# Attention and mixer's output: product A12 B21 first, block sums spread over the products, two-tensor operations on VectorE

## The chip, the cores and the metric

The kernel runs on one core of one Trainium2 chip. The metric is the time of one execution in microseconds, as the device measures it. The profile is of one execution; its engines are TensorE (PE, its weight loads PEld), VectorE (DVE), ScalarE (ACT), GpSimd (POOL) and SyncE (SP, which only issues transfers here).

## What is computed

A decoder trunk of two layers over 1024 positions of width 1024, all in float32. Each layer is a mixer, a cross-attention to 256 memory tokens and a SwiGLU FFN, and after each of the three stands a layer norm of the residual sum:

```python
def memory_cross_attention(x, mem_n, w_q, w_k, w_v, w_o):
    ...
    s = jnp.einsum('bshd,bmhd->bhsm', q, k).astype(jnp.float32) * (XA_DH ** -0.5)
    p = jax.nn.softmax(s, axis=-1).astype(x.dtype)
    o = jnp.einsum('bhsm,bmhd->bshd', p, v).reshape(B, S, D_MODEL)
    return o @ w_o

def swiglu_ffn(x, w_gate, w_up, w_down):
    return (jax.nn.silu(x @ w_gate) * (x @ w_up)) @ w_down

def reference(...):
    ...
    for l in range(DEPTH):
        if l % 2 == 0:
            ...
            y = hybrid_ab_mixer(x, ...)          # ends with y @ w_out
        else:
            ...
            y = multiscale_pool_mixer(x, ...)
        x = layer_norm(ALPHA * x + y, ln_mix_g[l], ln_mix_b[l])
        y = memory_cross_attention(x, mem_n, xa_wq[l], xa_wk[l], xa_wv[l], xa_wo[l])
        x = layer_norm(ALPHA * x + y, ln_xa_g[l], ln_xa_b[l])
        y = swiglu_ffn(x, ffn_wg[l], ffn_wu[l], ffn_wd[l])
        x = layer_norm(ALPHA * x + y, ln_ffn_g[l], ln_ffn_b[l])
    return x
```

## The kernel before, in words

**Precision.** Every operand of a product is split in two: a hi part, which ScalarE casts (L215, weights L123), and a lo part, the operand minus its hi part, a two-tensor subtraction on VectorE or GpSimd (L216, weights L125; `w.lo_engine` says which engine takes the weights' lo parts). One product is then three matmuls into the same bank (`mm3`, L210 to L212).

**Attention.** The kernel doesn't form q, k, v and o one by one. `build_A` multiplies the query weight with the memory's keys into a matrix A of 1024 x 1024, `attn_scores` multiplies x with it, a softmax follows, `build_VWo` multiplies the memory's values with the output weight, and `attn_out` multiplies the probabilities with that. So the scores, the attention's output and the mixer's output of the first layer are each a product of 1024 x 1024 by 1024 x 1024.

**Seven products.** Such a product is done in 2 x 2 blocks of 512 with seven block products in place of eight (`seven`, L807). With A blocks A11, A12, A21, A22 and B blocks in the same manner, product 1 is A11 B11, product 2 is A12 B21, and products 3 to 7 have block sums as operands (S1 to S4 of the A blocks, T1 to T4 of the B blocks). `ORDER_A` gives their order. A block is two pages of 128 x 1024, and a product has two halves g of one page of each side; a half product has 24 matmuls, 4 row tiles p of 6. `operands7` makes the hi and lo parts of each half product in that order, some three or four halves ahead, and `hook(j, g)`, called ahead of each half, issues the block sums (`combos_A`, `combos_B`), loads of x and layer-norm pieces.

**Banks.** The products accumulate in PSUM, in sets of four banks. Products 1, 6, 7 and 4 go on in one set (each adds to what stands there), 5 and 3 in another, and 2 in a set of its own. There are eight banks. So a new set needs banks of a finished one, and after each product the four results are added to the residual tiles x (L247 on VectorE; in the scores a VectorE addition or a ScalarE copy). Product 4 accumulates in the bank that product 7's addition has read, so it waits for that addition.

**Order.** Nothing is scheduled by a planner: the instructions stand on each engine's queue as the program emits them, and each engine does them in turn. `add` follows a product, `hook` precedes a half, and the operands' parts come between. The page pool has 44 pages; a page is taken again when its last reader is done.

**On which engine.** GpSimd takes the lo parts of A, many block sums (L732, L737, L741, L745, L757, L761), the weights' lo parts in the mixer's output, the attention's output and FFN-down, the softmax scaling of tiles 1 to 7 (L939; tile 0 has four VectorE operations, L942), and in FFN-down the affine step of tiles 4 to 6 (L1371, L1372). VectorE takes the lo parts of B, the other sums, the additions, and two operations for each tile of a layer norm (`ln_b`, L262 and L263). FFN-down has seven products too, in another order (`ORDER_D`) and with a different source for its operands; the first layer's weight transfers for it are issued by SyncE behind the stores of ScalarE that it waits for.

Of the kernel before, what the change touches and what calls it, by code (L numbers as in the profile page):

```python
# [15 lines left out]
P = 128  # L16
# [20 lines left out]
ORDER_A = (1, 2, 5, 6, 3, 7, 4)  # L37
ORDER_D = (1, 5, 6, 3, 7, 4, 2)

# [12 lines left out]
AFFINE = {(1, 2): ((0, "vector"), (4, "gpsimd")), (1, 3): ((1, "vector"),), (1, 4): ((2, "vector"), (5, "gpsimd")),  # L52
          (1, 5): ((3, "vector"),), (5, 1): ((6, "gpsimd"),), (5, 3): ((7, "vector"),)}
# [91 lines left out]
class Kern:  # L145
# [430 lines left out]
    def out_operands(self):  # L576

        A, B = {}, {}
        for k in (1, 2):
# [3 lines left out]
        A[1] = [self.Y[0, 0, g] for g in range(2)]  # L583
# [4 lines left out]
    def mixer0_out(self):  # L588
# [22 lines left out]
        def hook(j, g):  # L611
            if j == 1:
                if g == 0:
                    while self.y_ready[2] < 4:
                        self.pump()
                    A[2] = Y(0, 1)
# [25 lines left out]
        self.w.lo_engine = ("gpsimd",)  # L642
# [82 lines left out]
    def combos_A(self, A, step, eng):  # L725

        tt = eng.tensor_tensor
        if step == 0:
            (A11, A12), (A21, A22) = A["blocks"]
            S1 = [self.page("S1", [2, 512]) for _ in range(2)]  # L730
            for g in range(2):
                tt(S1[g], A21[g], A22[g], op=ALU.add)  # L732
            A.update({1: A11, 2: A12, 4: A22, 5: S1})
        elif step == 1:
            A11, S3 = A[1], A.pop("blocks")[1][0]
            for g in range(2):
                tt(S3[g], A11[g], S3[g], op=ALU.subtract)  # L737
            A[7] = S3
        elif step == 2:
            for g in range(2):  # L740
# [883 lines left out]
```

## Time and profile before

| | before |
|---|---|
| median of the runs | 2451.51 us (3 runs, 2450.9 to 2452.84) |
| profiled execution | 2451.65 us, its span 2449.9 us |
| mean granted clock of TensorE | 0.976 |
| busy: TensorE | 2312.4 us, 94% of the span |
| busy: VectorE, ScalarE, GpSimd | 1778.0, 1044.2 and 665.9 us |

How to read what follows: a time line gives the start of an instruction, its duration and, in brackets, how long its engine had stood idle before it and who ended that. A wait line gives the waiting engine's tile and line, the releaser, the us in total, the number of times and the longest. A window line gives the stretch, its us, the busy time (and instructions) of PE, PEld, DVE, ACT and POOL, the granted clock (1.00 is full), the DMA share and GB/s. A group of instructions has its busy time, the mean ns of one and the idle time before them. Short names: D is the set of banks of the seven products, dh and dl the hi and lo parts of their operands, S and T block sums, B a block of the right side, y and wp the mixer's left and right side, xf a block of x transposed, x a residual tile, wh and wl a weight's parts, pa and pk banks of `build_A` and the second mixer, xt a bank for transposes, s and hf sums of FFN-down's left side, p softmax tiles.

### The profile page before, as it was taken

How to read it: one execution, taken by the hardware profiler on the slowest of the kernel's cores; microseconds unless marked ns; L12 is line 12 of the kernel's file. 1: busy time of each engine (PE TensorE's matmuls, PEld its weight loads, DVE VectorE, ACT ScalarE, POOL GpSimd, SP SyncE). 2: the span in 40 equal slices, each digit the busy share in tenths (PEclk: the TensorE clock that was granted, in tenths of full speed). 3: DMA queues.
4: the chain of work that ended last, by engine and by line, in shares of the span. 5: the costliest groups of instructions: out<-in, count | busy, mean ns of one | idle time of the engine just before them, and what ended most of it. 6: DMA issues, size and time to landing. Idle time of an engine off the chain costs nothing. (4 is left out here: it accounts for less than half of the span.)

```text
span 2449.9 us, 29443 instructions
## 1 busy us (share of the span) xinstructions
PE 2312.4 (94%) x11208; PEld 1916.5 (78%) x11208; DVE 1778.0 (73%) x2126; ACT 1044.2 (43%) x1727; POOL 665.9 (27%) x401
## 2 busy tenths in 40 slices
PE   8999997797979999999999989798999999999998
PEld 7777776696868888888878789786788888887886
DVE  6986788868795876766774566978767667676555
ACT  3245555344736544444412234546364444342212
POOL 1332346757483000000110073755610000002001
PEclk9999999899989999999999999999999999999999
DMA  5111124050122234435796642302024353449783
GB/s 185 69 35 35 35 90 160 26 187 28 53 77 87 95 130 163 159 125 184 280 356 230 247 142 102 118 1 103 36 85 158 126 182 130 161 176 392 261 291 117
DMA packets 117341, 344.02 MB, mean 140 GB/s; under 512 B 10832, under 2 KB 11344, under 8 KB 117200
## 3 DMA queue, kind: packets, MB, share of 16 engines
q1 hardware_dynamic: 70560, 244.35, 27.7%
q10 hardware_dynamic: 46640, 97.79, 11.1%
q8 instruction: 89, 1.46, 0.2%
q14 instruction: 52, 0.43, 0.1%
HBM read 239.34 MB, written 102.76 MB: 140 GB/s over the span
## 5 line engine op out<-in xcount | busy, mean ns | idle before, releaser
L210 PE MATMUL P<-xh,op 128*128 128x512 f32 x1120 | 436.2, 389 | 2.1 <-ACT u L1301 2.1
L212 PE MATMUL P<-xh,op 128*128 128x512 f32 x1120 | 435.7, 389 | 0.0
L211 PE MATMUL P<-xl,op 128*128 128x512 f32 x1120 | 435.7, 389 | 0.0
L210 PE MATMUL D<-dh,dl 128*128 128x512 f32 x560 | 226.2, 404 | 58.4 <-DVE x L247 35.4
L1371 POOL TENSOR_TENSOR x<-x,lng 128x1024 f32<-128x1024 f32 x6 | 17.9, 2980 | 867.8 <-DVE s L1179 421.4
L210 PE MATMUL D<-dh,wp 128*128 128x512 f32 x616 | 242.4, 394 | 9.5 <-ACT dh L215 8.3
L210 PEld LDWEIGHTS P<-xh,op 128*128 128x128 f32 x1120 | 210.2, 188 | 47.3 <-ACT u L1301 3.8
L211 PE MATMUL D<-dl,wp 128*128 128x512 f32 x616 | 243.0, 395 | 3.3 <-DVE dl L216 3.3
L1113 DVE TENSOR_TENSOR op<-raw,op 128x512 fp32r<-128x512 f32 x200 | 137.9, 689 | 147.5 <-ACT op L1112 147.5
L212 PEld LDWEIGHTS P<-xh,op 128*128 128x128 f32 x1120 | 210.2, 188 | 44.0
L211 PE MATMUL D<-dl,dh 128*128 128x512 f32 x560 | 224.6, 401 | 21.1 <-DVE dl L216 21.1
L211 PEld LDWEIGHTS P<-xl,op 128*128 128x128 f32 x1120 | 210.2, 188 | 43.3
L212 PE MATMUL D<-dh,wp 128*128 128x512 f32 x616 | 241.8, 393 | 0.0
L212 PE MATMUL D<-dh,dh 128*128 128x512 f32 x560 | 223.4, 399 | 0.0
L125 POOL TENSOR_TENSOR wl<-raw,wh 128x1024 fp32r<-128x1024 f32 x64 | 173.5, 2723 | 164.3 <-ACT wh L123 159.9
L216 DVE TENSOR_TENSOR dl<-wp,dh 128x1024 fp32r<-128x1024 f32 x96 | 127.6, 1336 | 115.9 <-ACT dh L215 72.8
L215 ACT CAST dh<-wp 128x1024 fp32r<-128x1024 f32 x96 | 93.8, 989 | 265.4 <-DVE wp L777 57.3
L365 DVE SCALAR_TENSOR_TENSOR cacc<-sig,par,cacc 128x1023 f32<-128x1023 f32 (+14 forms) x120 | 175.5, 1462 | 2.5
L210 PEld LDWEIGHTS D<-dh,dl 128*128 128x128 f32 x560 | 108.8, 194 | 85.5 <-issue 36.6
L257 POOL TENSOR_SCALAR lst<-lst 128x1 f32<-128x1 f32 x48 | 27.3, 568 | 466.7 <-ACT sq L256 466.3
L216 POOL TENSOR_TENSOR dl<-xf,dh 128x1024 fp32r<-128x1024 f32 x48 | 141.5, 2965 | 39.6 <-ACT dh L215 29.2
L216 DVE TENSOR_TENSOR dl<-B,dh 128x1024 fp32r<-128x1024 f32 x48 | 117.9, 2488 | 40.7 <-ACT dh L215 40.7
(272 smaller groups left out, 5236.6 us busy)
## 6 DMA issues: line engine op xcount, KB each, us to landing
wp<-hD SPq DMA_DIRECT2D x140, 512.0 KB, 5.8
hD<-sh ACTq DMA_DIRECT2D x66, 512.0 KB, 3.8
raw<-in_wg SPq DMA_DIRECT2D x44, 512.0 KB, 4.2
raw<-in_wu SPq DMA_DIRECT2D x44, 512.0 KB, 3.3
hD<-hf ACTq DMA_DIRECT2D x44, 512.0 KB, 3.7
hD<-s ACTq DMA_DIRECT2D x44, 512.0 KB, 4.6
wp<-in_wd SPq DMA_DIRECT2D x40, 512.0 KB, 7.8
xD<-x ACTq DMA_DIRECT2D x32, 512.0 KB, 3.8
```

What stands on the lines that cost most here:

```text
L125: eng.tensor_tensor(lo, raw, hi.bitcast(F32), op=ALU.subtract)
L210: mm(out, ll, rh, start=start, stop=False, skip_group_check=more)
L211: mm(out, lh, rl, start=False, stop=False, skip_group_check=more)
L212: mm(out, lh, rh, start=False, stop=stop, skip_group_check=more)
L215: self.nc.scalar.copy(hi, src)
L216: getattr(self.nc, lo_engine).tensor_tensor(lo, src, hi.bitcast(F32), op=ALU.subtract)
L257: nc.gpsimd.tensor_scalar(st[:, 3:4], st[:, 3:4], 1.0 / D, LN_EPS, op0=ALU.mult, op1=ALU.add)
L365: nc.vector.scalar_tensor_tensor(acc[:, s:], u[:, :S - s], w[:, j:j + 1], acc[:, s:], op0=ALU.mult, op1=ALU.add)
L1113: getattr(nc, lo_engine).tensor_tensor(pg[:, 1], src, pg[:, 0].bitcast(F32), op=ALU.subtract)
L1371: eng.tensor_tensor(x[t], x[t], gx[0], op=ALU.mult)
```

## The change

`ORDER_A` begins with product 2 in place of product 1, and the residual's first term goes with it (`add_block` has an argument `early`, which FFN-down sets to 1 as before). The eight block sums have a table `SUMS`, which names the half product ahead of which each is issued: two operations of 128 x 1024 each, all on VectorE. No sum is issued while A or the value-output product is built. There the weight columns come in the order 4 to 7, 0 to 3, so that the blocks of product 2 are made first, and three halves of operands are made ahead. All lo parts of operands, the weights' lo parts in the three stages named, the softmax scaling and the affine step are on VectorE. VectorE's list goes from 2,021 rows to 2,189 and GpSimd's from 406 to 238; GpSimd keeps the weights' lo parts of the first mixer's projections and operations on single columns.

```diff
-ORDER_A = (1, 2, 5, 6, 3, 7, 4)
+ORDER_A = (2, 1, 5, 6, 3, 7, 4)
 ORDER_D = (1, 5, 6, 3, 7, 4, 2)
+
+SUMS = {(2, 1): "S1", (1, 0): "T1", (1, 1): "T2", (5, 0): "S2", (5, 1): "S3", (6, 0): "S4", (6, 1): "T3", (3, 1): "T4"}
...
-AFFINE = {(1, 2): ((0, "vector"), (4, "gpsimd")), (1, 3): ((1, "vector"),), (1, 4): ((2, "vector"), (5, "gpsimd")),
-          (1, 5): ((3, "vector"),), (5, 1): ((6, "gpsimd"),), (5, 3): ((7, "vector"),)}
+AFFINE = {(1, 2): (0, 4), (1, 3): (1,), (1, 4): (2, 5), (1, 5): (3,), (5, 1): (6,), (5, 3): (7,)}
...
         def hook(j, g):
-            if j == 1:
+            if j == 2:
...
-                B[("12", 3)[g]] = take2()
-                if g == 1:
-                    self.combos_B(B, 0, nc.vector)
-                    self.combos_B(B, 1, nc.gpsimd)
-            if j == 2 and g == 0:
+                B[(3, "12")[g]] = take2()
+            if j == 1 and g == 0:
                 while self.bg or self.bg2:
                     self.pump()
-                A["blocks"] = ((A[1], A[2]), (Y(1, 0), Y(1, 1)))
-                for i in range(3):
-                    self.combos_A(A, i, nc.vector)
-                self.combos_B(B, 2, nc.gpsimd)
-            if (j, g) in ((2, 1), (5, 0)):
+                A.update({"21": Y(1, 1), 4: Y(1, 0)})
+                self.block_sum(A, B, "S1")
+            if j != 2 and (j, g) in SUMS:
+                self.block_sum(A, B, SUMS[j, g])
+            if (j, g) in ((1, 1), (5, 0)):
                 load(4 + 2 * (j == 5))
                 load(5 + 2 * (j == 5))
-            if j == 6 and g == 0:
-                self.combos_B(B, 3, nc.vector)
-                self.combos_A(A, 3, nc.gpsimd)
...
-        self.w.lo_engine = ("gpsimd",)
+        self.w.lo_engine = ("vector",)
...
-    def operands7(self, order, fa, fb, ng, fast=()):
+    def operands7(self, order, fa, fb, ng):
         for j in order:
             for g in range(ng):
                 r = []
-                for f, eng in ((fa, "vector" if (j, g) in fast else "gpsimd"), (fb, "vector")):
+                for f in (fa, fb):
                     src = f(j, g)
                     hi, lo = self.page("dh", list(src.shape[1:]), F32R), self.page("dl", list(src.shape[1:]), F32R)
-                    self.split(hi, lo, src, eng)
+                    self.split(hi, lo, src)
...
-    def add_block(self, j, b, x0, x1, s0, s1):
+    def add_block(self, j, b, x0, x1, s0, s1, early=2):
...
-        x, st, eh, first = {1: (x0, None, 0, True), 2: (x0, s0, 0, False), 6: (x0, None, 1, True), 3: (x0, s0, 1, False),
+        x, st, eh, first = {early: (x0, None, 0, True), 3 - early: (x0, s0, 0, False), 6: (x0, None, 1, True), 3: (x0, s0, 1, False),
...
-        if pool:
-            nc.gpsimd.tensor_tensor(p, p, rs.unsqueeze(2).broadcast_to([P, HEADS, MEM]), op=ALU.mult)
-            return
         for h in range(HEADS):
             nc.vector.tensor_scalar(p[:, h, :], p[:, h, :], rs[:, h:h + 1], None, op0=ALU.mult)
...
         def attn(l):
-            for i in range(8):
+            for i in (4, 5, 6, 7, 0, 1, 2, 3):
                 w.add(a["wqT"][l, i], [8, P])
-            for i in range(8):
+            for i in (4, 5, 6, 7, 0, 1, 2, 3):
                 w.add(a["xa_wo"][l, i * P:(i + 1) * P, :], [D])
```

The new function that issues a sum, `block_sum(A, B, name)`, ends with two VectorE operations, one for each page:

```python
        for g in range(2):
            self.nc.vector.tensor_tensor(r[g], a[g], b[g], op=op)
```

In the order lists below, a line number of the changed kernel is one more for the same operation (L247 is L248, L216 is L217, L262 is L263), and L752 is a block sum there.

VectorE's list at the opening of the mixer's output, before: from the last of product 1's additions (x<-x,D) over three sums (two operations each, the second of each left out) and two lo parts to the additions of product 2.

```order
L247 SCALAR_TENSOR_TENSOR x_3513<-x_3513,D_514_3478 128x512
L732 TENSOR_TENSOR S_527_3561<-y_1538,y_3302 128x1024
...
L737 TENSOR_TENSOR y_1538<-y_1400,y_1538 128x1024
...
L741 TENSOR_TENSOR y_1400<-y_3302,y_1538 128x1024
...
L216 TENSOR_TENSOR dl_3580<-wp_435_3116,dh_3579 128x1024
L216 TENSOR_TENSOR dl_3616<-wp_461_3235,dh_3615 128x1024
L247 SCALAR_TENSOR_TENSOR x_3469,lst_3461<-x_3469,D_529_3571 128x512
L247 SCALAR_TENSOR_TENSOR x_3471,lst_3462<-x_3471,D_530_3572 128x512
L247 SCALAR_TENSOR_TENSOR x_3511,lst_3463<-x_3511,D_531_3573 128x512
L247 SCALAR_TENSOR_TENSOR x_3513,lst_3464<-x_3513,D_532_3574 128x512
```

The same place in the changed kernel: the additions are now those of product 2, the first of the stage.

```order
L217 TENSOR_TENSOR dl_3520<-y_3004,dh_3519 128x1024
L217 TENSOR_TENSOR dl_3524<-wp_480_3353,dh_3523 128x1024
L248 SCALAR_TENSOR_TENSOR x_3469<-x_3469,D_511_3475 128x512
L248 SCALAR_TENSOR_TENSOR x_3471<-x_3471,D_512_3476 128x512
L248 SCALAR_TENSOR_TENSOR x_3511<-x_3511,D_513_3477 128x512
L248 SCALAR_TENSOR_TENSOR x_3513<-x_3513,D_514_3478 128x512
L752 TENSOR_TENSOR S_525_3555<-y_3302,y_1538 128x1024
...
L752 TENSOR_TENSOR wp_470_3291<-wp_486_3372,wp_470_3291 128x1024
...
L217 TENSOR_TENSOR dl_3566<-S_525_3555,dh_3565 128x1024
L217 TENSOR_TENSOR dl_3570<-wp_470_3291,dh_3569 128x1024
L752 TENSOR_TENSOR T_535_3597<-wp_482_3364,wp_470_3291 128x1024
```

The six operations of sums that stood between the first and the second product's additions are gone from there; product 2's additions stand behind lo parts alone, and each sum comes between the lo parts of later halves.

VectorE's list at the end of the mixer's output, before: from product 3's last addition over two tiles' layer norm, one lo part, and two more tiles' to the first of product 7's additions (x_3607).

```order
L247 SCALAR_TENSOR_TENSOR x_3513,lst_3464<-x_3513,D_548_3654 128x512
...
L262 SCALAR_TENSOR_TENSOR x_3469<-x_3469,lst_3461,lng_3457 128x1024
L263 SCALAR_TENSOR_TENSOR x_3469<-x_3469,lst_3461,lnb_3458 128x1024
...
L216 TENSOR_TENSOR dl_3906<-wp_480_3353,dh_3905 128x1024
L262 SCALAR_TENSOR_TENSOR x_3511<-x_3511,lst_3463,lng_3457 128x1024
L263 SCALAR_TENSOR_TENSOR x_3511<-x_3511,lst_3463,lnb_3458 128x1024
L262 SCALAR_TENSOR_TENSOR x_3513<-x_3513,lst_3464,lng_3457 128x1024
L263 SCALAR_TENSOR_TENSOR x_3513<-x_3513,lst_3464,lnb_3458 128x1024
L247 SCALAR_TENSOR_TENSOR x_3607,lst_3465<-x_3607,D_511_3475 128x512
```

The same place in the changed kernel.

```order
L256 TENSOR_SCALAR lst_3464<-lst_3464 128x1
L263 SCALAR_TENSOR_TENSOR x_3469<-x_3469,lst_3461,lng_3457 128x1024
L264 SCALAR_TENSOR_TENSOR x_3469<-x_3469,lst_3461,lnb_3458 128x1024
...
L126 TENSOR_TENSOR wl_578_3892<-raw_3473,wh_577_3891 128x1024
L217 TENSOR_TENSOR dl_3902<-y_2644,dh_3901 128x1024
L217 TENSOR_TENSOR dl_3906<-wp_461_3235,dh_3905 128x1024
L263 SCALAR_TENSOR_TENSOR x_3511<-x_3511,lst_3463,lng_3457 128x1024
L264 SCALAR_TENSOR_TENSOR x_3511<-x_3511,lst_3463,lnb_3458 128x1024
L263 SCALAR_TENSOR_TENSOR x_3513<-x_3513,lst_3464,lng_3457 128x1024
L264 SCALAR_TENSOR_TENSOR x_3513<-x_3513,lst_3464,lnb_3458 128x1024
L126 TENSOR_TENSOR wl_584_3938<-raw_3515,wh_583_3937 128x1024
L248 SCALAR_TENSOR_TENSOR x_3601,lst_3465<-x_3601,D_527_3561 128x512
```

Between the additions of product 3 and of product 7 stand three operations more: the A side's lo part (dl<-y) and two weights' lo parts (wl).

VectorE's list at the start of the first score stage, before: sums of the B blocks, then the lo parts of four half products' B side, then the first VectorE additions to the score tiles p.

```order
L752 TENSOR_TENSOR B_4434<-B_4436,B_4434 128x1024
...
L757 TENSOR_TENSOR T_691_4742<-B_4582,B_4434 128x1024
...
L761 TENSOR_TENSOR B_4436<-B_4582,B_4436 128x1024
...
L216 TENSOR_TENSOR dl_4757<-B_4580,dh_4756 128x1024
L216 TENSOR_TENSOR dl_4789<-B_4581,dh_4788 128x1024
L216 TENSOR_TENSOR dl_4833<-B_4434,dh_4832 128x1024
L216 TENSOR_TENSOR dl_4865<-B_4435,dh_4864 128x1024
L971 TENSOR_TENSOR p_4816<-D_709_4824,p_4816 128x512
```

The same place in the changed kernel, from the first sum of the stage on.

```order
L752 TENSOR_TENSOR S_697_4768<-xf_4293,xf_4295 128x1024
...
L217 TENSOR_TENSOR dl_4773<-xf_4153,dh_4772 128x1024
L217 TENSOR_TENSOR dl_4777<-B_4577,dh_4776 128x1024
L752 TENSOR_TENSOR B_4576<-B_4578,B_4576 128x1024
...
L217 TENSOR_TENSOR dl_4819<-S_697_4768,dh_4818 128x1024
L217 TENSOR_TENSOR dl_4823<-B_4576,dh_4822 128x1024
L752 TENSOR_TENSOR T_715_4850<-B_4436,B_4576 128x1024
...
L217 TENSOR_TENSOR dl_4855<-S_698_4769,dh_4854 128x1024
L217 TENSOR_TENSOR dl_4859<-B_4577,dh_4858 128x1024
L947 TENSOR_TENSOR p_4804<-D_707_4814,p_4804 128x512
```

The sums stood together, ahead of the lo parts; now each pair of sums is followed by the two lo parts (A's and B's) of one half product or of two.

## Rows read from the trace of the kernel before

**Rows 1.** The page's engines: busy us (share of the span) x instructions

```profile
PE 2312.4 (94%) x11208; PEld 1916.5 (78%) x11208; DVE 1778.0 (73%) x2126; ACT 1044.2 (43%) x1727; POOL 665.9 (27%) x401
```

**Rows 2.** TensorE's waits: line, releaser, us in total, times, longest

```profile
PE D L210 <- DVE x L247: 35.4, 6, 14.8
PE D L211 <- DVE dl L216: 24.4, 7, 10.6
PE D L210 <- POOL dl L216: 23.0, 5, 9.6
PE D L210 <- ACT dh L215: 8.3, 2, 4.1
PE pk L210 <- POOL wl L125: 6.1, 3, 5.7
PE pa L210 <- DVE wl L125: 2.9, 2, 1.5
PE pa L210 <- POOL wl L125: 1.7, 1, 1.7
PE xt L272 <- ACT B L1020: 2.1, 2, 1.1
```

**Rows 3.** Windows: FFN-up, then stages in the text's order, last a start

```profile
826.32:1208.94 382.62, 381.56 (x1682) 315.32 (x1681) 274.19 (x401) 168.59 (x281) 0.00 (x0) 1.00 0.46 164
394.72:503.49 108.77, 80.59 (x340) 65.27 (x339) 92.37 (x85) 40.29 (x53) 78.94 (x37) 0.87 0.18 65
559.51:649.96 90.45, 78.42 (x339) 64.26 (x338) 73.51 (x54) 40.66 (x66) 56.70 (x19) 0.94 0.06 19
1567.46:1659.01 91.55, 79.51 (x339) 65.06 (x338) 73.53 (x54) 40.66 (x66) 56.71 (x19) 0.93 0.06 18
680.82:767.26 86.44, 73.31 (x305) 59.33 (x304) 72.22 (x67) 34.16 (x39) 58.43 (x32) 0.92 0.11 43
1689.87:1777.23 87.36, 73.28 (x305) 59.40 (x303) 71.52 (x67) 34.09 (x39) 58.46 (x32) 0.90 0.11 43
1208.78:1428.39 219.61, 213.06 (x925) 174.55 (x923) 133.85 (x142) 53.17 (x60) 31.10 (x21) 0.98 0.73 269
1241.66:1248.46 6.80, 4.99 (x11) 3.62 (x12) 4.72 (x4) 1.69 (x2) 0.00 (x0) 0.50 1.03 413
```

**Rows 4.** Timelines of the first score stage: start us, us, operation

```profile
573.61 6.04 DVE L757 TENSOR_TENSOR T<-B,B 128x1024 f32<-128x1024 f32 x2
579.57 2.35 DVE L761 TENSOR_TENSOR B<-B,B 128x1024 f32<-128x1024 f32 x2
568.66 6.63 POOL L216 TENSOR_TENSOR dl<-xf,dh 128x1024 fp32r<-128x1024 f32 x2
```

**Rows 5.** VectorE's timeline, mixer's output, opening

```profile
407.62 2.47 DVE L247 SCALAR_TENSOR_TENSOR x<-x,D 128x512 f32<-128x512 f32 x4
416.66 6.68 DVE L737 TENSOR_TENSOR y<-y,y 128x1024 f32<-128x1024 f32 x2
427.68 4.49 DVE L216 TENSOR_TENSOR dl<-wp,dh 128x1024 fp32r<-128x1024 f32 x2
```

**Rows 6.** Timelines of VectorE and TensorE, mixer's output, products 7 and 4

```profile
468.25 1.28 DVE L262 SCALAR_TENSOR_TENSOR x<-x,lst,lng 128x1024 f32<-128x1024 f32 x1
476.78 3.39 DVE L262 SCALAR_TENSOR_TENSOR x<-x,lst,lng 128x1024 f32<-128x1024 f32 x1
490.76 0.77 PE L210 MATMUL D<-dh,dl 128*128 128x512 f32 x1 [12.53 <-DVE x L247]
```

**Rows 7.** Costliest groups on VectorE: softmax scaling of tile 0, an FFN operation

```profile
L942 DVE TENSOR_SCALAR p<-p,rs 128x256 f32<-128x256 f32 x8 | 2.3, 349 | 0.1
L1169 DVE TENSOR_TENSOR s<-s,sh 128x1024 fp32r<-128x1024 f32 x44 | 53.4, 1218 | 0.0
```

**Rows 8.** Timelines of VectorE and GpSimd, start of the first FFN-down

```profile
1210.18 2.89 DVE L1180 TENSOR_TENSOR s<-hf 128x512 f32<-128x512 f32 x1
1209.94 2.59 POOL L1371 TENSOR_TENSOR x<-x,lng 128x1024 f32<-128x1024 f32 x1 [420.87 <-DMA lng<-in_ln_xa_g]
```

More of the change, by code (lines that the diff above doesn't have):

```diff
@@ L578, in out_operands @@
         A, B = {}, {}
-        for k in (1, 2):
+        for k in (2, 1):
             B[k] = [self.w.take() for _ in range(2)]
@@ L582, in out_operands @@
             self.pump()
-        A[1] = [self.Y[0, 0, g] for g in range(2)]
+        A[2] = [self.Y[0, 0, g] for g in range(2)]
         self.sides = A, B
@@ L709, in mem_v @@
         self.M = None
[L725 to L740, printed above, removed]
-                tt(A[1][g], A[4][g], A[7][g], op=ALU.subtract)
-            A[6] = A[1]
-        else:
-            for g in range(2):
-                tt(A[6][g], A[2][g], A[6][g], op=ALU.subtract)
-            A[3] = A[6]
@@ L748, in combos_B, with block_sum @@
-    def combos_B(self, B, step, eng):
-        tt = eng.tensor_tensor
-        if step == 0:
-            for g in range(2):
-                tt(B[1][g], B["12"][g], B[1][g], op=ALU.subtract)
-            B[5] = B[1]
-        elif step == 1:
-            B[6] = [self.page("T2", [2, 512]) for _ in range(2)]
-            for g in range(2):
-                tt(B[6][g], B[3][g], B[5][g], op=ALU.subtract)
-        elif step == 2:
-            B[7] = B.pop("12")
-            for g in range(2):
-                tt(B[7][g], B[3][g], B[7][g], op=ALU.subtract)
-        else:
-            for g in range(2):
-                tt(B[2][g], B[2][g], B[6][g], op=ALU.subtract)
-            B[4] = B[2]
+    def block_sum(self, A, B, name):
+        new = lambda: [self.page(name, [2, 512]) for _ in range(2)]
+        if name == "S1":
+            r, a, b, op = new(), A["21"], A[4], ALU.add
+            A[5] = r
+        elif name == "S2":
+            r, a, b, op = A[1], A[5], A[1], ALU.subtract
+            A[6] = r
+        elif name == "S3":
+            r, a, b, op = A.pop("21"), A[4], A[6], ALU.subtract
+            A[7] = r
+        elif name == "S4":
+            r, a, b, op = A[2], A[2], A[6], ALU.subtract
+            A[3] = r
+        elif name == "T1":
+            r, a, b, op = B[1], B["12"], B[1], ALU.subtract
+            B[5] = r
+        elif name == "T2":
+            r, a, b, op = new(), B[3], B[5], ALU.subtract
+            B[6] = r
+        elif name == "T3":
+            r = B.pop("12")
+            a, b, op = B[3], r, ALU.subtract
+            B[7] = r
+        else:
+            r, a, b, op = B[2], B[2], B[6], ALU.subtract
+            B[4] = r
+        for g in range(2):
+            self.nc.vector.tensor_tensor(r[g], a[g], b[g], op=op)
@@ L888, in build_A @@
         self.made = []
-        for dc in range(DC):
-            if dc in (0, 2) and self.AT[dc // 2] is None:
-                self.scores_T(dc // 2)
-            if dc % 4 == 0:
+        for n in range(DC):
+            dc = (n + 4) % DC
+            if n in (0, 2) and self.AT[n // 2] is None:
+                self.scores_T(n // 2)
+            if n % 4 == 0:
                 for k in ((1, "12"), (2, 3))[dc // 4]:
@@ L946, in softmaxes @@
         live = []
-        todo = [self.softmax(self.Pm[t], t in (1, 2, 3, 4, 5, 6, 7)) for t in ts]
+        todo = [self.softmax(self.Pm[t]) for t in ts]
         while todo or live:
@@ L996, in build_VWo @@
         rest = self.softmaxes(range(4, NT))
-        for h in range(HEADS):
-            if h == 3:
+        for i in range(HEADS):
+            h = (i + 2) % HEADS
+            if i == 3:
                 self.w.split_ahead = 1
-            if h % 2 == 0:
+            if i % 2 == 0:
                 for k in ((1, "12"), (2, 3))[h // 2]:
@@ L1004, in build_VWo @@
             for mc in range(2):
[L1005 removed]
+                if i == 0 and mc == 0:
                     next(self.first)
```

75 lines of the change are left out of this document (26 added, 49 removed).

## Prediction

> **What bounds the kernel now.** I read the page's engine table first, then the waits of TensorE, then windows cut at the stages, and last the timelines of VectorE and GpSimd around the longest waits. TensorE is busy for 94% of the span, VectorE for 73%, GpSimd for 27% [rows 1]. So the time is TensorE's own work plus the places where it stands still. The waits say who ends those: additions of a product to the residual (x, L247) 35.4 us, lo parts on VectorE 24.4, lo parts on GpSimd 23.0, hi parts of the FFN's last product 8.3, weight lo parts 6.1 and 2.9 [rows 2]. Nearly all of it lies in the stages that the diff touches.
>
> The windows size that. In a stretch without stalls TensorE does 1,680 matmuls in 382.62 us, 0.2278 us each [rows 3]. Seven products of 48 matmuls take 336 x 0.2278 = 76.5 us. The mixer's output takes 108.77, an excess of 32.2. The two score stages take 90.45 and 91.55: excess 13.9 and 15.0. The two attention outputs take 86.44 and 87.36; their windows hold 300 of the matmuls (68.3 us), so 18.1 and 19.0. The first FFN-down has 924 matmuls (210.5 us) in 219.61: 9.1. The granted clock belongs to this excess: after the stall at the start of FFN-down it is 0.50 for 6.8 us [rows 3], the lower of its two levels (1.2 of 2.4 GHz), and the mean of the mixer's output is 0.87 against 1.00 in the stretch without stalls. So the first matmuls after a stall run at half pace.
>
> Why the stages stall is read off single instructions. Two VectorE operations on two SBUF tensors of 128x1024 take 6.04 us beside a GpSimd operation of the same kind and 2.35 right after it has ended, in one stage [rows 4]; GpSimd's own take 3.3 each there. Four residual additions, with one input in PSUM, take 2.47 while GpSimd works [rows 5], about 0.61 each. So one operation on each engine costs some 3.3 us, and two in a row on VectorE about 2.3 (I take 1.14 each in a list, a little under half of 2.35, since the second begins before the first has ended). Splitting these operations over two engines makes them slower than one engine would.
>
> **The change part by part.**
>
> *Mixer's output, opening.* Product 5 waited 14.8 us, the longest of the L247 waits [rows 2], for the banks of product 2, whose additions stood behind six sums (a pair takes 6.68 beside GpSimd), the last ending near 427.7, and two lo parts, 4.49 [rows 5]. Now product 2 comes first, its four additions come right after two lo parts, and its banks are free while product 1 runs. That wait goes, 14.8 us of the 32.2.
>
> *Mixer's output, end.* Product 4 waited 12.53 us [rows 6] for the additions of product 7, behind layer-norm halves that took 3.39 instead of 1.28 us [rows 6]. What is late next is VectorE itself. From the first addition of product 2 to the first of product 7 its list holds 38 two-tensor operations (16 of the sums, 20 lo parts, 2 weight lo parts), 8 layer-norm halves and 20 additions: 38 x 1.14 + 8 x 1.28 + 20 x 0.61 = 65.8 us, and some 0.8 for small ones, 66.6. TensorE has five products in that time, 54.6 us. So product 4 still waits, 12.0 us by this count; I take 11.5, as the list can begin a little before product 2 has ended, and 1.8 for half clock behind it (6.8 us at half pace lose 3.4 [rows 3]; part of that lies inside the wait). Excess 13.3 instead of 32.2: gain 18.9. Bounds: 32 if a better order inside the list lets product 7's additions pass (no stall), 10 if VectorE loses 0.15 us or so per operation in starts.
>
> *Score stages.* TensorE waited 10.55 us for B's lo, queued behind sums made at once before the stage [rows 2, 4]. The sums now come one per half product and GpSimd does none. VectorE's list in the stage is 38 two-tensor operations and 12 additions, 43.3 + 7.3 = 51 us against 76.5 of TensorE, so it stays ahead. Gain 13.9 + 15.0 = 28.9; bounds 20 (if the first product still waits for lo parts behind the last weight splits) and 28.9.
>
> *Attention outputs.* The 9.6 us waits for GpSimd's lo parts go [rows 2]. From product 2's additions to product 7's VectorE has 34 operations and 20 additions, 52 us against 54.6: just enough. ScalarE's chain of squares, normalisations and casts behind product 3 can hold the last lo parts, which stand ahead of product 7's additions: I take 3 us left in each, clock included, out of 18.1 and 19.0. Gain 31.1; bounds 22 and 37.
>
> *Building A and the value-output product.* TensorE waited twice for weight lo parts on VectorE, 2.9 us, slowed by GpSimd's sums, and once, 1.7, for one on GpSimd [rows 2]; these go, 4.6 us; bounds 0 and 4.6. In the second the softmax scaling of 14 tiles moves from one GpSimd operation to four VectorE operations; eight of these take 2.3 us [rows 7], so 1.15 us a tile, in front of the copies that free the transposes' banks. TensorE waits there up to 1.1 us already [rows 2]; I charge 1.5 us for each layer, 3 us. Bounds 0 and 6.
>
> *FFN-down.* The longest gap, 4.1 us [rows 2], ends with a weight whose transfer was issued late: two sums before it took 2.89 us each on VectorE beside two GpSimd operations [rows 8]. Like the sums without company they should take 0.7, so the stores and the transfers behind them go out 4.4 us earlier. But the affine step of three tiles, 2 operations each, now takes 2.28 us a tile of VectorE's list. I take 4 of the 9.1 us per layer, 8 in all; bounds 0 (the DMA share there is 1.03 [rows 3], so the transfer may land no earlier) and 14.
>
> *At no cost.* The halves of the weights swap places in their queue, same transfers, same order of use, nothing else on that queue passes them. The loads of x on SP's queue move from one half product to the next and are wanted one product later. Which product is the first into x changes no operation. The weight lo parts that move to VectorE in the second mixer replace a 5.7 us wait [rows 2] with VectorE's 1.2 us after about the same chain: nothing counted, bounds 0 and 3.
>
> The sum: 18.9 + 28.9 + 31.1 + 4.6 + 8 - 3 = 88.5 us. The profiled execution took 2451.65 us with a span of 2449.9; the median of the runs is 2451.51, the same within 0.01%. 2451.65 - 88.5 = 2363.
>
> The Trainium skill weighs in on whether unloading GpSimd on a full VectorE can pay. Its page "Perfetto Trace Analysis", section "Optimizing Scalar/DVE Operations", says that where VectorE is saturated it may make sense to offload to ScalarE or even GpSimd, and adds that the two share an SBUF read port, so that moving work between them might not help. In the mixer's output VectorE is saturated, and by the first half of the rule some of the 66.6 us should stay on GpSimd. If ten of them could leave for nothing, the wait at product 4 would go and the sum be about 2350. The trace bears out the second half: an operation left there adds about 2.2 us to a neighbour on VectorE and takes away 1.14, so the wait would grow.
>
> **The rivals.**
>
> *A. VectorE becomes the bound more widely.* Everything two-tensor is now in one list with ScalarE's casts feeding it. If each of the lists loses 0.15 to 0.25 us per operation to waits for casts and pages, mixer's output keeps 20 to 22 us of excess, the attention outputs 8 each, the scores 2, and the FFN gains nothing: 2363 + 8 + 10 + 4 + 8 = 2393. For it: in mixer's output VectorE has no slack at all. Against: TensorE's waits name no cast of ScalarE outside FFN-down [rows 2].
>
> *B. No stall left.* If product 7's additions come in time, mixer's output and the attention outputs run at pace: 2363 - 13.3 - 6 = 2344. Against: the count of 66.6 against 54.6 us.
>
> *C. Slower: the 3.4 us are not GpSimd's doing.* If VectorE's two-tensor operations are slow for another reason (TensorE reading the same memory, say), they stay slow when GpSimd is silent, and the lists are longer. With c us per operation the excesses are 46c - 41 in the mixer's output, 34c - 41.4 in each attention output and 38c - 69.2 in each score stage, 190c - 262 in all, against 98 before. It decides at c = 1.9; at c = 2.3, half way, the stages lose 77 and the other parts give 10: 2519. Against: 44 operations of this size in the FFN, where TensorE never rests and GpSimd does nothing [rows 3], take 1.218 each [rows 7], and the change of pace within one stage [rows 4].
>
> *D. The transfers or the chain keep the gaps.* If only half of the removed waits go because other producers (ScalarE's casts, weights) are late behind them, 44 us: 2407.
>
> **How the numbers follow.** Forecast (2350 to 2380) 0.52, A 0.21, B 0.12, D 0.09, C 0.04; 0.02 for no change, if the waits are simply replaced. The range goes from just below B, 2341, to just above D, 2409: it leaves out C, no change and the outer ends of B and D. A measurement of this kernel can tell about 0.2%, 5 us: faster 0.94, same 0.02, slower 0.04.
>
> **What would show it.** Right: no wait for L247 additions ahead of product 5; one wait of 10 to 13 us ahead of product 4 in the mixer's output; VectorE's lo parts at 1.22 in every group; GpSimd's busy time down from 666 us to about 200, since weights' lo parts of the first mixer and single columns are left to it; score windows of 77 us; the clock at full pace in them. Wrong: two-tensor operations at 2 us or more with GpSimd idle (C); waits of TensorE for ScalarE's casts or for lo parts in the score stages (A, D); the 4.1 us gap unchanged.

## The result and the profile after

The changed kernel takes 2383.85 us (median of 4 runs, 2383.04 to 2385.47) against 2451.48 for the kernel before in the same comparison: a ratio of 0.9724, 95% interval 0.9707 to 0.9741. That is 67.6 us gained, where 88.5 were forecast. The time lies inside the range, some 21 us above the predicted 2363 and above the 2350 to 2380 to which the forecast gave a chance of 0.52. The profiled execution took 2383.61 us with a span of 2381.8.

The page's engines after, beside [rows 1]:

```profile
PE 2302.4 (97%) x11208; PEld 1911.7 (80%) x11208; DVE 1756.4 (74%) x2336; ACT 1043.4 (44%) x1727; POOL 191.3 (8%) x233
```

GpSimd went from 665.9 to 191.3 us, yet VectorE, which took over its operations, went down, from 1778.0 to 1756.4. TensorE's waits after (line, releaser, us in total, times, longest), beside [rows 2]:

```profile
PE D L211 <- DVE x L248: 18.9, 3, 11.4
PE D L211 <- ACT dh L216: 7.5, 2, 4.3
...
PE pk L211 <- DVE wl L126: 6.4, 1, 6.4
...
PE D L212 <- DVE dl L217: 4.3, 10, 1.5
PE xt L273 <- ACT B L996: 3.2, 2, 1.6
PE xt L273 <- DVE B L994: 3.0, 2, 1.5
...
PE xt L273 <- DVE kl L217: 2.3, 1, 2.3
```

The waits of D for lo parts, 47 us on two engines, are down to 4.3. The additions still end three waits, and the transposes (xt) wait longer than before, in one place for a lo part kl of the memory's product. The windows after, in the order of [rows 3] (stretch, its us, busy us of PE, PEld, DVE, ACT and POOL, granted clock, DMA share, GB/s):

```profile
393.09:483.92 90.83, 79.40 (x340) 65.20 (x339) 83.28 (x108) 39.97 (x53) 9.57 (x13) 0.92 0.23 77
540.87:617.22 76.35, 76.35 (x339) 63.23 (x338) 66.43 (x80) 40.13 (x66) 0.00 (x0) 1.00 0.08 24
1522.98:1599.34 76.36, 76.36 (x339) 63.24 (x338) 66.44 (x80) 40.13 (x66) 0.00 (x0) 1.00 0.08 25
649.64:724.51 74.87, 71.05 (x301) 58.22 (x302) 66.16 (x87) 34.30 (x39) 3.55 (x12) 0.96 0.19 71
1634.37:1708.00 73.63, 70.02 (x301) 57.45 (x302) 65.23 (x86) 34.30 (x39) 3.55 (x12) 0.98 0.18 67
1166.41:1388.39 221.98, 214.34 (x927) 174.62 (x926) 131.48 (x151) 53.05 (x60) 4.44 (x12) 0.98 0.74 269
```

Against [rows 3]: the mixer's output 108.77 to 90.83, the score stages 90.45 and 91.55 to 76.35 and 76.36 (TensorE busy all the time, clock 1.00), the attention outputs 86.44 and 87.36 to 74.87 and 73.63, the first FFN-down 219.61 to 221.98, longer than before.

The end of the mixer's output, VectorE's timeline after (start us, us, operation), beside [rows 6]:

```profile
454.26 1.28 DVE L263 SCALAR_TENSOR_TENSOR x<-x,lst,lng 128x1024 f32<-128x1024 f32 x1
...
466.81 1.29 DVE L264 SCALAR_TENSOR_TENSOR x<-x,lst,lnb 128x1024 f32<-128x1024 f32 x1
468.01 1.22 DVE L126 TENSOR_TENSOR wl<-raw,wh 128x1024 fp32r<-128x1024 f32 x1
469.14 0.68 DVE L248 SCALAR_TENSOR_TENSOR x<-x,D 128x512 f32<-128x512 f32 x1
```

No row between these has an idle time in brackets: VectorE is full, its operations at 1.22 and 1.28 us, and product 7's first addition starts at 469.14. From product 2's first addition, at 401.46, that is 67.7 us, 0.7 of them idle. The products begin at 393.09 and TensorE goes on at 469.98 after 11.43 us.

### The profile page after: what moved, and what is told of

The parts are those of the page before. It is cut to its first block, busy times and chain, and to the rows that moved or that the text cites. A ratio compares the mean times of both kernels' runs of the same rounds, so it can differ in the third digit from the quotient of the medians.

```text
span 2381.8 us, 29275 instructions
## 1 busy us (share of the span) xinstructions
PE 2302.4 (97%) x11208; PEld 1911.7 (80%) x11208; DVE 1756.4 (74%) x2336; ACT 1043.4 (44%) x1727; POOL 191.3 (8%) x233
## 3 DMA queue, kind: packets, MB, share of 16 engines
q10 hardware_dynamic: 46640, 97.79, 11.4%
## 5 line engine op out<-in xcount | busy, mean ns | idle before, releaser
L211 PE MATMUL D<-dh,dl 128*128 128x512 f32 x560 | 221.3, 395 | 19.0 <-DVE x L248 18.9
L216 ACT CAST dh<-wp 128x1024 fp32r<-128x1024 f32 x96 | 93.6, 989 | 277.1 <-DVE wp L764 66.0
L217 DVE TENSOR_TENSOR dl<-wp,dh 128x1024 fp32r<-128x1024 f32 x96 | 109.9, 1146 | 119.4 <-ACT dh L216 79.1
L212 PEld LDWEIGHTS D<-dl,wp 128*128 128x128 f32 x616 | 116.8, 190 | 34.6 <-DVE dl L217 10.8
L211 PEld LDWEIGHTS D<-dh,wp 128*128 128x128 f32 x616 | 116.8, 190 | 34.5 <-ACT dh L216 8.3
L1265 ACT COPY u<-P 128x512 f32<-128x512 f32 x120 | 70.6, 588 | 161.9 <-PE P L213 161.9
L213 PEld LDWEIGHTS D<-dh,wp 128*128 128x128 f32 x616 | 116.8, 190 | 24.1
```

What stands on the lines that cost most here:

```text
L211: mm(out, ll, rh, start=start, stop=False, skip_group_check=more)
L212: mm(out, lh, rl, start=False, stop=False, skip_group_check=more)
L213: mm(out, lh, rh, start=False, stop=stop, skip_group_check=more)
L216: self.nc.scalar.copy(hi, src)
L217: getattr(self.nc, lo_engine).tensor_tensor(lo, src, hi.bitcast(F32), op=ALU.subtract)
L1265: nc.scalar.copy(u[j], b)
```

## The experiments

The theory: a two-tensor operation on VectorE and one on GpSimd cost more side by side than one after the other on VectorE, and that, not the order, is most of the gain; what is missing from the forecast is in three places that were sized wrongly. The rival: the order of products and the spreading of the sums bring the gain, and the missing part is VectorE's full list everywhere.

**e1_order**: the new order, engines about as before.

```diff
-                for f in (fa, fb):
+                for f, eng in ((fa, "gpsimd"), (fb, "vector")):
...
-            self.nc.vector.tensor_tensor(r[g], a[g], b[g], op=op)
+            (self.nc.gpsimd if name[0] == "S" else self.nc.vector).tensor_tensor(r[g], a[g], b[g], op=op)
...
-        self.w.lo_engine = ("vector",)
+        self.w.lo_engine = ("gpsimd",)
```

> The changed kernel's order of products, spread of the sums and order of weight columns, with the engines about as before: A's lo parts, the four S sums, the weights' lo parts of the three stages, the softmax scaling of tiles 1 to 7 and the affine step of tiles 4 to 6 on GpSimd. Theory (the gain comes from two-tensor operations no longer running beside each other on two engines): operations stay at 2.4 to 3.4 us, of the 67.7 us gained only the 14.8 us wait of product 5 and little more is there: 2415 to 2450 us. Rival (the order and the spreading of the sums bring the gain, wherever the operations run): 2380 to 2400 us.

Measured 2437.7 us, ratio 0.9943 (0.9923 to 0.9963): 14 us of the 67.6. With the order alone product 5's wait is gone, but product 4 now waits 17.6 us where it waited 12.53 [rows 6]:

```profile
PE D L211 <- DVE x L248: 34.1, 3, 17.6
```

VectorE's lo parts of B (busy us, mean ns) in the kernel before, in this run and in the changed kernel show why:

```profile
L216 DVE TENSOR_TENSOR dl<-B,dh 128x1024 fp32r<-128x1024 f32 x48 | 117.9, 2488 | 40.7 <-ACT dh L215 40.7
...
L217 DVE TENSOR_TENSOR dl<-B,dh 128x1024 fp32r<-128x1024 f32 x48 | 115.0, 2408 | 49.5 <-ACT dh L216 49.3
...
L217 DVE TENSOR_TENSOR dl<-B,dh 128x1024 fp32r<-128x1024 f32 x48 | 58.6, 1220 | 0.0
```

In this run they still take about twice the 1.220 us of the changed kernel.

**e2_engine**: the old order, all those operations on VectorE.

```diff
-                    self.combos_B(B, 1, nc.gpsimd)
+                    self.combos_B(B, 1, nc.vector)
...
-                for f, eng in ((fa, "vector" if (j, g) in fast else "gpsimd"), (fb, "vector")):
+                for f, eng in ((fa, "vector"), (fb, "vector")):
```

> The kernel before in its own order, product 1 first and the sums where they stood, with every two-tensor operation that the change moves put on VectorE. Theory (engines): all these operations fall to 1.22 us; the wait of product 5 for product 2's additions shrinks from 14.8 to 4 to 8 us, since six or eight sums still stand ahead of them; the score stages keep some of their wait, because the sums still come in one piece ahead of the lo parts; 2390 to 2410 us. Rival (order): most of the gain is missing, over 2430 us.

Measured 2408.2 us, ratio 0.9822 (0.9803 to 0.9842): 43.6 of the 67.6 us. The same group has fallen to 1.216 us:

```profile
L216 DVE TENSOR_TENSOR dl<-B,dh 128x1024 fp32r<-128x1024 f32 x48 | 58.4, 1216 | 0.0
```

Product 5 waits 7.8 us in place of 14.8, and the score stages keep 4.7 us each, because the sums still come in one piece:

```profile
PE D L210 <- DVE x L247: 22.6, 4, 7.8
PE D L210 <- DVE dl L216: 9.4, 2, 4.7
```

So the engine alone is two thirds of the gain, the order alone a fifth; the remaining 10 us need both. Once the engine is changed, the order is worth 24.3 us more. The rival falls for most of it.

**e3_ffn_loads**: a transfer question. In FFN-down four loads of x go out later:

```diff
-            if j == 1 and g < 4:
-                for t in (g, g + 4):
+            if j == 1:
+                for t in (g,) if g < 4 else (2 * g - 4, 2 * g - 3):
...
+AFFINE = {(1, 2): (0,), (1, 3): (1,), (1, 4): (2,), (1, 5): (3,), (5, 1): (4,), (5, 2): (5,), (5, 3): (6,), (5, 4): (7,)}
```

> The changed kernel, with the four loads of the residual tiles 4 to 7 in FFN-down issued two to four half products later and their affine steps behind them; nothing else. These are 2.1 MB that went out among the first weights of the stage. Theory (the first gap there, 4.3 and 3.2 us, is bound by the transfers: they land one behind the other every 1.25 us, so stores that go out earlier land no earlier): the weight that ends the gap lands about 5 us earlier, the gap shrinks below 1 us, the half clock behind it goes, 2371 to 2378 us. Rival (the gap is made by the chain of VectorE sums, ScalarE stores and SyncE's wait for them): gap unchanged, 2384 us.

In the changed kernel VectorE's sums at the start of FFN-down are at 0.69 us, as forecast against the 2.89 of [rows 8], and two of ScalarE's stores (hD<-hf) go out 1.9 and 2.5 us earlier in the stage. But SyncE's next transfer, which starts when the second of them has landed, starts 16.7 us into the stage (1183.12), where it started 16.3 us in before; from 1164 to 1200 the DMA engines move 387 GB/s on average, most of the time 400 to 420. VectorE's and SyncE's timelines of the changed kernel, and the window up to the gap, with a DMA share of 1.01:

```profile
1167.81 0.69 DVE L1144 TENSOR_TENSOR s<-hf 128x512 f32<-128x512 f32 x1
...
1183.12 0.82 SPq L97 DMA_DIRECT2D wp<-hD  x2
...
1198.39 1.23 DVE L764 TENSOR_TENSOR wp<-wp,wp 128x1024 f32<-128x1024 f32 x1 [5.10 <-DMA wp<-in_wd]
...
1166.40:1200.00 33.60, 30.09 (x133) 24.59 (x131) 19.82 (x21) 7.55 (x9) 0.00 (x0) 0.99 1.01 385
```

The run also moves the affine steps of those tiles. They are not what the gap waits for: just ahead of its end VectorE stands idle for 5.10 us until a weight has landed, and the cast and the lo part follow on that sum. In this run the same transfer of SyncE starts 13.9 us into the stage:

```profile
1179.27 0.83 SPq L97 DMA_DIRECT2D wp<-hD  x2
```

With the loads later the 4.3 us wait of the first layer is gone, no wait in that part of the stage is longer than 0.88, and the clock stays at 1.00:

```profile
1165.38:1383.73 218.35, 212.59 (x927) 172.89 (x926) 131.74 (x151) 53.05 (x60) 4.45 (x12) 1.00 0.73 273
```

The stage goes from 221.98 to 218.35 us, the second one by 1.1. Measured 2379.8 us, ratio 0.9706 (0.9689 to 0.9722), not told apart from the changed kernel's by the intervals; the stage's window is what decides. The gap was bound by transfers. The excess over 210.5 us is still 7.9: small waits, most of them for lo parts (0.4 to 0.9), stand behind the place of the long one, and 1.5 us late in the stage that was there all along. In most half products behind that place VectorE does a sum, a lo part and an affine step and waits in between for ScalarE's cast, in all some 6 us against 5.44 of TensorE's matmuls.

**e4_lnn_later**: in the attention output, two normalisations behind the last casts.

```diff
-            if j == 7:
-                self.ln_n(x[2 * g], sts[2 * g])
-                self.ln_n(x[2 * g + 1], sts[2 * g + 1])
+            if j == 7 and g == 1:
+                for t in range(4):
+                    self.ln_n(x[t], sts[t])
```

> The changed kernel, with the first two normalisations of the attention output issued one half product later, so that ScalarE's casts of the last operands stand ahead of them. Theory (product 4 waits because ScalarE's squares, two normalisations and casts delay the last lo part, which stands ahead of product 7's additions on VectorE): the lo part comes some 2.5 to 3.5 us earlier, the waits of 3.8 and 3.6 us fall below 1 us, 2374 to 2379 us in all. Rival (VectorE's own list is too long, 52 us counted against 54.6 and it is nearer): waits shrink by under 1 us, 2382 to 2385 us.

In the changed kernel VectorE stands idle for 7 us just ahead of product 7's additions, and ScalarE's cast ends that. Ahead of the cast stand four squares and two normalisations, which wait 1.10 us for columns from GpSimd:

```profile
712.59 2.38 ACT L270 ACTIVATE x<-x,lst 128x1024 f32<-128x1024 f32 x2 [1.10 <-POOL lst L269]
...
714.87 1.03 ACT L216 CAST dh<-xf 128x1024 fp32r<-128x1024 f32 x1
...
715.94 1.23 DVE L217 TENSOR_TENSOR dl<-xf,dh 128x1024 fp32r<-128x1024 f32 x1 [6.99 <-ACT dh L216]
```

In this run the same operation has waited 3.52 us:

```profile
714.96 1.23 DVE L217 TENSOR_TENSOR dl<-xf,dh 128x1024 fp32r<-128x1024 f32 x1 [3.52 <-ACT dh L216]
```

and both stages run at pace, 68.92 and 68.68 us for 300 matmuls:

```profile
652.17:721.09 68.92, 68.60 (x302) 56.46 (x303) 63.86 (x85) 32.99 (x38) 5.58 (x12) 1.00 0.14 54
1631.11:1699.79 68.68, 68.54 (x302) 56.45 (x303) 62.96 (x84) 32.94 (x38) 5.58 (x12) 1.00 0.14 54
```

Measured 2374.0 us, ratio 0.9681 (0.9666 to 0.9695), below the changed kernel's interval. VectorE's list there was not too long; ScalarE's chain was. The rival falls at this place.

**e5_lnb_later**: in the mixer's output, the layer norm of four tiles behind product 7's additions.

```diff
-            if j == 7:
+            if j == 4:
                 self.ln_b(x[2 * g], sts[2 * g], gb)
```

> The changed kernel, with the layer-norm operations of the first four residual tiles in the mixer's output issued behind product 7's additions instead of ahead of them. Theory (product 4 waits 11.4 us because VectorE's list between product 2's and product 7's additions, 66.6 us, is longer than five products, 54.6): 8 operations of 1.28 us fewer there, the wait falls to 1 to 2 us, the stage from 90.8 to 78 to 80 us; some of it may come back as a wait of the memory's value product behind it, 2.3 us before, up to 5; 2371 to 2376 us. Rival (the wait hangs on ScalarE's casts or the weights' lo parts there): the wait falls by less than 5 us, 2379 us or more.

The wait at product 4 falls from 11.4 to 4.67 us, not to 1 or 2: VectorE now idles 3.52 us for a weight's cast, which stands behind ScalarE's squares:

```profile
457.59 1.23 DVE L126 TENSOR_TENSOR wl<-raw,wh 128x1024 fp32r<-128x1024 f32 x1 [3.52 <-ACT wh L124]
```

What is won comes back behind the stage. Windows of the mixer's output and of the stretch from there to the first scores:

```profile
392.83:476.99 84.16, 79.49 (x340) 65.22 (x339) 77.69 (x96) 34.88 (x45) 2.96 (x8) 0.96 0.19 70
476.99:541.12 64.13, 55.15 (x448) 54.51 (x448) 47.63 (x63) 36.65 (x53) 4.96 (x8) 0.92 0.55 189
```

Together 148.3 us; in the changed kernel 90.83 and 56.95, together 147.8. TensorE's transposes now wait 9.0 us, 2.3 in the changed kernel, for kl, a lo part of the memory's product. VectorE is not full there: it stands idle for 3.76 us until ScalarE has cast kh, and ScalarE issues six stores of x ahead of that cast:

```profile
PE xt L273 <- DVE kl L217: 9.0, 2, 7.2
...
493.43 0.42 DVE L217 TENSOR_TENSOR kl<-pk,kh 128x256 fp32r<-128x256 f32 x1 [3.76 <-ACT kh L216]
...
489.21 3.77 ACTq L862 DMA_DIRECT2D xD<-x  x3
```

The cast starts at 493.02; in the changed kernel it starts at 492.55, although the mixer's output ends 6.9 us later there. Measured 2385.8, ratio 0.9731 (0.9715 to 0.9748): no gain. So the theory holds for the wait and fails for the time. VectorE's list still brings ScalarE's last square at the same time (487.18, in the changed kernel 486.72), and behind it come the stores and the cast; which of these holds the time was not tested by itself.

**e6_softmax_pool**: the softmax scaling of tiles 1 to 7 back on GpSimd.

```diff
+        if p is not self.Pm[0]:
+            nc.gpsimd.tensor_tensor(p, p, rs.unsqueeze(2).broadcast_to([P, HEADS, MEM]), op=ALU.mult)
+            return
```

> The changed kernel, with the softmax scaling of tiles 1 to 7 back on GpSimd as one operation a tile. Theory (the waits of the transposes, 1.6 and 1.5 us in each layer where 1.07 stood before, and the longer value-output product of the second layer come from these operations in VectorE's queue ahead of the copies): 30.9 us between the scores and the attention output instead of 32.4 and 35.0; 2378 to 2381 us. Rival (the new order of heads and the weights' lo parts make them): unchanged, 2384 us, or more, if GpSimd's operation slows VectorE's two-tensor ones beside it.

Measured 2376.6 us, ratio 0.9693 (0.9679 to 0.9708). The stretches between scores and attention output were 32.42 and 35.03 us in the changed kernel and are 30.79 and 30.75, as in the kernel before (30.86). The windows of the changed kernel, then of this run:

```profile
617.22:649.64 32.42, 29.22 (x160) 24.63 (x159) 28.36 (x54) 27.59 (x66) 0.00 (x0) 1.00 0.39 139
1599.34:1634.37 35.03, 31.84 (x161) 26.63 (x160) 29.66 (x55) 27.59 (x66) 0.00 (x0) 0.90 0.36 128
...
614.44:645.23 30.79, 29.24 (x161) 24.63 (x159) 26.75 (x34) 27.36 (x66) 10.67 (x6) 1.00 0.42 153
1593.33:1624.08 30.75, 29.31 (x161) 24.78 (x159) 26.59 (x34) 27.21 (x66) 10.84 (x6) 1.00 0.43 152
```

The transposes' waits for copies (B) fall from 6.2 us in four to 2.9 in four, as in the kernel before (2.8):

```profile
PE xt L273 <- ACT B L999: 2.2, 2, 1.1
PE xt L273 <- DVE B L997: 0.7, 2, 0.3
```

So this one part of the change costs 5.9 us; the rest of the 7.2 us between the medians lies in places this edit does not touch.

**e7_all and e9_three**: e3, e4, e5 and e6 together, and the same without e5.

> The changed kernel with the four moves together: loads of tiles 4 to 7 later in FFN-down, normalisations later in the attention output, layer norm later in the mixer's output, softmax scaling of tiles 1 to 7 on GpSimd. If the four places are independent, 2384 less 4, 10, 8 to 12 and 3 to 6 us: 2352 to 2359 us. If VectorE's list is full behind the mixer's output too, 2358 to 2365 us.

> The changed kernel with three of the four moves: loads of tiles 4 to 7 later in FFN-down, normalisations later in the attention output, softmax scaling of tiles 1 to 7 on GpSimd; the layer norm of the mixer's output stays ahead of product 7's additions. Theory (moving that layer norm only shifts VectorE's full list from the wait at product 4 into the memory's value product, and with the shorter stages costs a little): 2360 to 2364 us, some 2 to 5 us below all four moves (2365.5), the wait at product 4 11.4 us again, the stretch from the mixer's output to the first scores 55 us. Rival (the four moves add up): 2366 to 2370 us.

Measured 2365.5 us (0.9648, 0.9633 to 0.9662) and 2364.8 us (0.9646, 0.9633 to 0.966): the same. Both expectations of a difference missed; the layer norm's place does not matter, as e5 said. These versions beat the changed kernel by 19 us, and the sum of e3, e4 and e6 alone (4.1, 9.8 and 7.2, together 21.1) accounts for it within the spread of the runs.

**e10_weights**: beyond e9, in the first FFN-down, four weights of the next stage split at once.

```diff
-                if layer < DEPTH - 1 and p < 2:
-                    self.w.ahead(2 * p + 2, 2 * p + 4)
+                if layer < DEPTH - 1 and p == 0:
+                    self.w.ahead(4, 6)
```

> As the run before, and in the first FFN-down the four weights of the memory's keys are split ahead of the last product's second addition rather than two by two. Theory (the 6.4 us wait at the start of the second mixer is not a matter of the engine that makes the weight's lo part, since it was 5.7 us with GpSimd: its hi part, a cast, stands behind a square on ScalarE that waits for a norm): the wait falls below 2 us and its half clock goes, 5 to 9 us less than without this step. Rival (the lo part itself is late on VectorE, or the weight's transfer is): the wait stays over 5 us, same time.

Measured 2364.6 us (0.9647, 0.9634 to 0.966), no gain, and the wait is 6.09 us: the theory's forecast of under 2 us failed. TensorE does the first four weights' products and then waits for the fifth, whose cast on ScalarE comes behind the last square. The edit moved the wrong weights, so it tells only that the first four were not what the wait hung on; whether a fifth weight made earlier would end it was not tried.

**e8_probe**: idle GpSimd operations beside FFN-up.

```diff
+            if k == 0:
+                pool.tensor_tensor(d[0], g, d[1], op=ALU.mult)
+            elif k == 1:
+                pool.tensor_scalar(d[0], g, 1.0, 0.0, op0=ALU.mult, op1=ALU.add)
+            elif k == 2:
+                pool.tensor_tensor(d[0].rearrange("p (a b) -> p a b", a=4), g.rearrange("p (a b) -> p a b", a=4),
+                                   d[1][:, 0:4].unsqueeze(2).broadcast_to([P, 4, P]), op=ALU.mult)
```

> The changed kernel, with 24 idle GpSimd operations of 128x512 of each of three forms added in the first FFN-up, where GpSimd otherwise does nothing and TensorE never rests: a product of two SBUF tensors, a scaling with constants, a product with one column per block of 128 spread over it (the form of the softmax scaling). One page fewer in the page pool. Theory (VectorE's two-tensor operations are slow only beside a GpSimd operation that reads tensors of its own): VectorE's 128x512 two-tensor operations rise from 0.69 to 1.3 us or more beside the first form, and to as much or nearly beside the second; beside the third, where the trace of before showed no slowing, under 0.8. Rival (any work on GpSimd slows them the same): all three forms alike. With TensorE ahead of its operands the time of FFN-up stays 382.6 us within 2.

VectorE's operations of 128x512 with both inputs in SBUF, 0.69 us alone, beside the three forms in turn:

```profile
808.64 1.78 DVE L1096 TENSOR_TENSOR op<-raw,op 128x512 fp32r<-128x512 f32 x1
...
930.24 1.09 DVE L1096 TENSOR_TENSOR op<-s,op 128x512 fp32r<-128x512 f32 x1
...
1044.51 1.52 DVE L1096 TENSOR_TENSOR op<-s,op 128x512 fp32r<-128x512 f32 x1
```

And one of 128x1024, 1.22 us alone, beside the three forms in turn:

```profile
810.35 2.31 DVE L1152 TENSOR_TENSOR s<-s,sh 128x1024 fp32r<-128x1024 f32 x1
...
925.10 1.63 DVE L1152 TENSOR_TENSOR s<-s,sh 128x1024 fp32r<-128x1024 f32 x1
...
1077.86 2.06 DVE L1152 TENSOR_TENSOR s<-s,sh 128x1024 fp32r<-128x1024 f32 x1
```

All three forms slow VectorE, by different amounts: 1.09, 0.40 and 0.83 us on the short operation, 1.09, 0.41 and 0.84 on one twice as long. The theory's numbers missed twice, the third form is not free, and the second costs less than thought; the rival, all alike, is wrong too. FFN-up took 388.8 us where 382.6 within 2 was expected: a 3.3 us wait for an operand at its start, and a shorter one. The probe had one page fewer in the pool and one run, so that time is no measure of contention.

## Why the prediction was right or wrong

The time is inside the range, and not because errors cancelled. By the terms of the sum the gain fell short by 1.0 us in the mixer's output, 5.8 in the attention outputs, 1.0 at building A, 2.7 in the value-output product and 9.9 in FFN-down, and was 0.4 above in the scores: 20 us together. Of its signs of being right all came true; of those of being wrong one did, the 4.1 us gap stayed.

- **Product 5's wait** went entirely, as forecast: between 393.09 and 469.98 TensorE has one idle stretch, the one ahead of product 4.
- **Product 4's wait** was put at 11.5 us from 66.6 us of list against 54.6 of products; measured 11.43, from 67.7 us of list. The stage gained 17.9, forecast 18.9. e5 adds what the prediction did not see: taking operations out of that list ends most of the wait and gains nothing, because the next wait takes its place.
- **Score stages**: 14.1 and 15.2 us gained, forecast 13.9 and 15.0.
- **Attention outputs**: 11.6 and 13.7 us, forecast 31.1 together. The mechanism was named, ScalarE's chain ahead of the last lo part; the term was mis-sized, 3 us left in each against 6.6 and 5.3 measured. VectorE waited 6.99 us for that cast, of which product 4 felt 3.8, and half clock followed. e4 takes nearly all of it away: in the first layer a wait of 0.3 us is left.
- **Value-output product**: charged 3 us, measured 1.6 and 4.2, in all 5.7, inside the bound of 6. In the second layer half clock followed the two waits (0.90 over the stretch against 1.00 in the first). e6 shows that it is the softmax scaling.
- **FFN-down** is the step that failed, with the sign wrong: forecast 8 us gained, measured 2.4 lost in the first layer and 0.5 gained in the second. The sums on VectorE did shrink by 4.4 us, and two stores went out 1.9 and 2.5 us earlier; they landed no earlier, because the DMA engines were full (a share of 1.01 up to the gap). The row that said so, a DMA share of 1.03 [rows 3], was read as one end of a bound when it was the answer; e3 shows it. The transfers explain why nothing was gained, not what was lost: the gap is only 0.2 us longer than before. Behind it five half products take 29.5 us (1206.70 to 1236.23) where they took 27.2 (1248.85 to 1276.08), and from the gap to there VectorE's list has the affine steps of five tiles where it had those of three. The stage takes 221.60 us in e2, with these steps and the weights' lo parts on VectorE, and 220.22 in e1, with them on GpSimd. So the loss is most likely the price of operations that moved to VectorE, the affine step among them, which the prediction named and sized too small; no run tests it by itself.
- **Building A**: 4.6 us forecast; the stretch from the first FFN-down to the second scores became 4.5 us shorter, but that from the mixer's output to the first scores 0.9 longer (56.02 to 56.95). The waits for weights' lo parts went in both; in the first layer there is a new wait of 2.3 us, with half clock behind it, for a lo part kl that stands on VectorE behind two layer-norm operations and a wait for ScalarE's cast. It was not in the sum.
- **The rivals**: A was near in time (2393) for half a reason: VectorE is the bound in the mixer's output, but its operations lost next to nothing each, and in the attention outputs it was one wait for ScalarE. Against A the prediction held that TensorE's waits name no cast of ScalarE outside FFN-down; that was a misreading, as the waits before have one in the first mixer (PE gate L210 <- ACT xh L215: 6.2, 2, 4.7). B, no stall left (2344), was not reached even by e9 (2364.8), where product 4's wait still stands at 11.4. C, slowness that is not GpSimd's, is refuted by e2: 1.216 us with the old order. D, other producers late behind the waits, is what happened in FFN-down and in part in the attention outputs, but its 44 us was too low for the whole.

The Trainium skill's page "Perfetto Trace Analysis", section "Optimizing Scalar/DVE Operations", says that offloading from a saturated VectorE to GpSimd may make sense and might not help. Both halves are borne out here: e2 against the kernel before shows 43.6 us gained by taking two-tensor operations off GpSimd, e6 5.9 us gained by giving the softmax scaling back to it, in stretches where VectorE is busy 28.4 of 32.4 and 29.7 of 35.0 us and does copies, reductions and column scalings.

## What to carry to other kernels

Before splitting work over VectorE and GpSimd, look at one operation's time alone and beside the other engine: here a pair cost 3.3 us on two engines and 2.3 on VectorE alone. Before moving an operation from ahead of one wait to behind it, follow the path into the next stage: here the next wait took over all that was won. And where a transfer ends a wait, look first at how full the DMA engines are in that stretch: with a DMA share of 1.01 an earlier store gained nothing here, fewer bytes ahead of it did.

## What the runs showed of the hardware

The amount by which a GpSimd operation lengthens a VectorE operation on two SBUF tensors does not depend on the latter's length: 0.69 became 1.78 and 1.22 became 2.31 beside the first form, 1.09 us more each time; beside the scaling it was 0.40 and 0.41, beside the spread column 0.83 and 0.84. A VectorE operation that began 0.40 us into a GpSimd operation of the first form was lengthened less, to 1.44:

```profile
814.07 1.29 POOL L1076 TENSOR_TENSOR dum<-sg,dum 128x512 f32<-128x512 f32 x1 [2.49 <-ACT sg L1190]
814.47 1.44 DVE L1096 TENSOR_TENSOR op<-s,op 128x512 fp32r<-128x512 f32 x1 [1.21 <-ACT op L1095]
```

This looks like taking turns rather than running at half speed, one GpSimd operation let through for each VectorE operation. The kernel before fits: twice the 1.09 of the first form, for twice the elements, and the 1.14 of VectorE in a list make 3.3 us, and that is what a 128x1024 pair took. That it is turns was read off these durations, not tested by itself. A column spread over a block in place of a second tensor lowers the price (0.83), a constant lowers it more, none makes it free.
